# Output stores of the first four token tiles go into the queue six steps later

## The chip, the cores and the metric

The kernel runs on one core of one Trainium2 chip. The metric is the device time of one execution in microseconds; lower is better. Before the change the median of three runs is 2676.28 us, the runs lying from 2673.13 to 2678.49 us. All arithmetic is in fp32; every large matrix product is split into high and low fp32r parts and issued as three matmuls.

## The reference, cut to what matters

One transformer layer on 1024 latent tokens and 256 context tokens, width 1024: a half-step SwiGLU, two parallel attentions with a gated output projection, and a second half-step SwiGLU. The change touches the very last piece, the down projection of the second SwiGLU and the residual step that writes the output:

```python
def _rmsnorm(x, g):
    x32 = x.astype(jnp.float32)
    y = x32 * lax.rsqrt(jnp.mean(x32 * x32, axis=-1, keepdims=True) + RMS_EPS)
    return y.astype(x.dtype) * g

def _residual(x, y, g_post, gate, weight):
    return x + weight * gate * _rmsnorm(y, g_post)

def _swiglu(h, w1, w3, w2):
    return (jax.nn.silu(h @ w1) * (h @ w3)) @ w2
...
        x = _residual(x, _swiglu(_modnorm(x, g[4], m[6], m[7]), ffn2_w1[l], ffn2_w3[l], ffn2_w2[l]),
                      g[5], m[8], HALF_STEP)
    return x
```

## The kernel before, in words

The program is fully unrolled. It is written as a list of *steps* (class `Plan`): each step has one main piece of work, mostly matmuls, and side pieces that `plan.spread` hangs on chosen steps. All that a step issues is recorded in that order, and since nearly every instruction is pinned, each engine runs its own instructions in exactly the recorded order. An instruction that has to wait holds up whatever stands behind it on the same engine.

All transfers, loads and stores alike, go through one queue, SP's. `ld` puts a load at the end of the queue at once. `store(dst, src, n)` does not: it notes the store and puts it into the queue at the end of the step that comes `n` steps later (`flush` does this after each step).

The last phase is the second SwiGLU's down projection, class `Down7`: 77 products, each a 128-deep slice of one of seven sums (a Strassen-Winograd scheme with seven blocks of 11 products). Products 0 to 71 are steps *o* to *o*+71 here. Each has four groups of three matmuls of 128x512, one group per PSUM bank (the names `bs`, `bm`, `bv`). The last five products, 72 to 76, are done bank by bank in four tail steps. Called "product *i*" below, each needs:

- a load of two tiles of 128x512 (named `t`, from scratch tensors `d`), put into the queue six steps ahead (`load`); for products 72 to 76 this is at steps *o*+59, 61, 63, 65 and 67. The `t` tiles come from a pool of 20 slots.
- a split of both tiles (`split`) three steps ahead: ScalarE (ACT) casts the high part into `xu`, VectorE (DVE) subtracts for the low part. For products 72 to 76 this is at steps *o*+62, 64, 66, 68 and 70.

At the end of a block of 11 products `out` adds the banks into the result tiles `ys` (name `xv`) on DVE. Block 4 ends with step *o*+54, block 5 with *o*+65; blocks 5 and 6 gather in the same four banks.

After step *o*+54 the rows of token tiles 0 to 3 are complete, and `done2(t, 0)` and `done2(t, 1)` finish them at steps *o*+55+2t and *o*+56+2t. The first loads the residual rows of the tile from scratch tensor `x2s` into a 128x1024 tile (`xr` in the code, `xv<-d` in a profile), computes the row's inverse norm (a square with a sum on ACT, two tiny operations on POOL) and multiplies by the gate row on DVE (`z`). The second does one DVE SCALAR_TENSOR_TENSOR, z times the inverse norm plus `xr`, and stores z to `out` (`out_x<-xv`). Token tiles 4 to 7 follow in the same way in the tail steps.

Of the kernel before, what the change touches and what calls it, by code (L numbers as in the profile page):

```python
# [15 lines left out]
P = 128  # L16
# [27 lines left out]
def hybrid_block(ctx: ExitStack, tc: tile.TileContext, a: dict, out: bass.AP):  # L44
# [25 lines left out]
    def V(dt=F32):  # L70
        return U(dt, "v")
# [50 lines left out]
    def ld(dst, src):  # L122
        for x in [x for x in waiting if x[1].tensor.name == src.tensor.name]:
            waiting.remove(x)
            put(*x[1:])
        return put(dst, src)
# [4 lines left out]
    def put(dst, src):  # L131
        return pin(nc.sync.dma_start(dst, src))  # L132

    def store(dst, src, n=2):

        if clock[0] is None:
            return put(dst, src)
        waiting.append((clock[0] + n, dst, src))
# [218 lines left out]
    def rstd(src, n):  # L357
        junk = T2(BF16, 1024)
        ss = ST()
        act.activation(junk[:, :n], src, AF.Square, accum_out=ss)  # L360
        r = ST()
        pool.tensor_scalar(ss, ss, 1.0 / n, EPS, op0=ALU.mult, op1=ALU.add)
        pool.tensor_tensor(r, ss, mhalf[:, 0:1], op=ALU.pow)
        return r
# [703 lines left out]
    o = len(plan.main)  # L1068
# [57 lines left out]
    o = len(plan.main)  # L1126
# [6 lines left out]
    for i, d in enumerate(downs):  # L1133
        last = i == len(downs) - 1
        o = len(plan.main)
# [18 lines left out]
        if i < len(downs) - 2:  # L1154
            n = downs[i + 1]
            plan.spread([lambda n=n: n.loads(n.fs[0])], o, o + 1)
            plan.spread(n.steps(), o + 3, e)
        elif not last:
            n = downs[i + 1]
# [87 lines left out]
    o = len(plan.main)  # L1247
# [144 lines left out]
    o = len(plan.main)  # L1392
# [5 lines left out]
    for x, (c, s, ts) in enumerate(sets):  # L1398
        o = len(plan.main)
# [211 lines left out]
    o = va_at  # L1611
# [10 lines left out]
    o = len(plan.main)  # L1622
# [3 lines left out]
    o = len(plan.main)  # L1626
# [4 lines left out]
    o = len(plan.main)  # L1631
# [3 lines left out]
    o = len(plan.main)  # L1635
# [379 lines left out]
    for d in range(KD):  # L2015
        o = len(plan.main)
# [51 lines left out]
    o = len(plan.main)  # L2068
# [13 lines left out]
    o = len(plan.main)  # L2082
# [14 lines left out]
    o, tail = down2.plan(plan)  # L2097
# [8 lines left out]
    def done2(t, x):  # L2106
        y = ys2[t]
        if x == 0:
            xr, r, z = V(), rstd(y, D), V()
            ld(xr, x2s[t * P:(t + 1) * P, :])  # L2110
            vec.tensor_tensor(z, y, cols["g8"], op=ALU.mult)
            cols[t] = xr, r, z
        else:
            xr, r, z = cols[t]
            n = 512 if t == 7 else D
            for o in range(0, D, n):
                vec.scalar_tensor_tensor(z[:, o:o + n], z[:, o:o + n], r, xr[:, o:o + n], op0=ALU.mult, op1=ALU.add)
                store(out[t * P:(t + 1) * P, o:o + n], z[:, o:o + n], 0)

    plan.spread(ada_steps((8,)), o + 1, o + 2 * NP - 3)  # L2120
    plan.spread([last_col], o + 2 * NP - 3, o + 2 * NP - 2)
# [1 line left out]
    for t in range(4):  # L2123
        plan.spread([lambda t=t, x=x: done2(t, x) for x in range(2)], o + 5 * NP + 2 * t, o + 5 * NP + 2 * t + 2)
        plan.spread([lambda t=t: done2(t + 4, 0)], tail + t, tail + t + 1)
        plan.spread([lambda t=t: done2(t + 4, 1)], min(tail + t + 1, tail + 3), tail + 4)
# [79 lines left out]
```

## Time and profile before

| What | Value |
|---|---|
| Median of three runs | 2676.28 us |
| Profiled execution, its own time | 2674.99 us |
| Span of that execution, first to last instruction | 2672.9 us |
| PE (TensorE matmuls) busy | 2612.1 us, 98% of the span |
| DVE busy | 1847.6 us, 69% |
| ACT busy | 1173.5 us, 44% |
| POOL busy | 229.5 us, 9% |
| Mean granted TensorE clock | 0.992 |

Times are in microseconds from the start of the span. Engine rows give when an instruction, or a run of alike ones, begins and how long it lasts; in square brackets stands the idle time of the engine ahead of it, and the engine and tile whose work ended that idle time. `SPq` rows are the moments at which SP issues a transfer, not the transfer itself. DVE instructions overlap a little in the record, so what one costs in a row of them is the distance between starts.

### The profile page before, as it was taken

What the parts mean: (1) busy time and instruction counts of PE and PEld (TensorE: products, weight loads), DVE (VectorE), ACT (ScalarE), POOL (GpSimd) and SP (SyncE); (2) the same over time, 40 slices, a digit from 0 to 9 for tenths busy, and PEclk for the clock granted to TensorE, in tenths of its full rate; (3) what the DMA queues carried; (4) which work ended last, traced back from release to release, by engine and by line L of the source; (5) the groups of instructions that cost most, each with busy time, mean ns of one, the idle gap of its engine ahead of it and who ended that gap; (6) DMA issues with size and microseconds to landing.
All of it is one profiled execution on the core that took longest, in us unless ns stands there. A gap on an engine that the chain in (4) does not pass through costs nothing. (4 is left out here: it accounts for less than half of the span.)

```text
span 2672.9 us, 38325 instructions
## 1 busy us (share of the span) xinstructions
PE 2612.1 (98%) x13690; PEld 2235.5 (84%) x13690; DVE 1847.6 (69%) x3495; ACT 1173.5 (44%) x2248; POOL 229.5 (9%) x380
## 2 busy tenths in 40 slices
PE   7999999999999999999999999999999999999997
PEld 5888888888888788789888999997788888888885
DVE  4777875586866676665466988886525788777555
ACT  4532223532223663331346988774246322234533
POOL 0000000000000400000102432221011000000001
PEclk9999999999999999999999999999999999999998
DMA  7454433453433564477789942214325566557645
GB/s 288 154 165 144 143 117 114 143 169 107 167 109 107 196 229 155 158 245 237 216 285 275 254 115 74 74 30 172 108 87 186 196 229 224 181 186 268 225 162 200
DMA packets 220430, 460.58 MB, mean 172 GB/s; under 512 B 25488, under 2 KB 64592, under 8 KB 220240
## 3 DMA queue, kind: packets, MB, share of 16 engines
q1 hardware_dynamic: 220240, 458.14, 52.2%
q8 instruction: 108, 1.77, 0.3%
q14 instruction: 82, 0.67, 0.1%
HBM read 338.71 MB, written 119.34 MB: 171 GB/s over the span
## 5 line engine op out<-in xcount | busy, mean ns | idle before, releaser
L153 PE MATMUL bm<-xu,xu 128*128 128x512 f32 (+1 forms) x2271 | 553.9, 388 | 1.4 <-DVE xu L120 1.1
L153 PEld LDWEIGHTS bm<-xu,xu 128*128 128x128 f32 x2271 | 420.2, 189 | 84.2 <-DVE xu L120 1.9
L153 PE MATMUL bs<-xu,xu 128*128 128x512 f32 (+1 forms) x1875 | 462.5, 386 | 10.6 <-DVE xv L120 8.5
L120 ACT CAST xu<-t 128x512 fp32r<-128x512 f32 x402 | 239.5, 618 | 407.4 <-DVE t L120 333.7
L153 PEld LDWEIGHTS bs<-xu,xu 128*128 128x128 f32 x1875 | 348.3, 189 | 79.1 <-issue 8.9
L120 DVE TENSOR_TENSOR xu<-t,xu 128x512 fp32r<-128x512 f32 x402 | 265.8, 686 | 142.8 <-ACT xu L120 142.8
L153 PE MATMUL bs<-xv,xu 128*128 128x512 f32 (+1 forms) x1488 | 356.0, 389 | 5.1 <-DVE t L120 5.0
L153 PEld LDWEIGHTS bs<-xv,xu 128*128 128x128 f32 x1488 | 279.5, 189 | 62.9 <-issue 7.1
L153 PE MATMUL bv<-xv,xu 128*128 128x512 f32 x1276 | 318.5, 389 | 0.0
L153 PEld LDWEIGHTS bv<-xv,xu 128*128 128x128 f32 x1276 | 239.5, 188 | 49.9
L120 POOL TENSOR_SCALAR st<-st 128x1 f32<-128x1 f32 x72 | 39.4, 547 | 2089.1 <-ACT t L120 2029.3
L153 PE MATMUL bs<-w,w 96*128 96x512 f32 (+3 forms) x832 | 206.1, 366 | 7.7 <-DVE st L1725 7.1
L120 DVE TENSOR_TENSOR xu<-xu,xu 128x512 fp32r<-128x512 f32 (+2 forms) x219 | 149.3, 687 | 76.9 <-ACT xu L120 75.2
L153 PE MATMUL bm<-t,xu 128*128 128x256 f32 (+1 forms) x1272 | 167.4, 289 | 0.6 <-ACT t L120 0.4
L153 PEld LDWEIGHTS bm<-t,xu 128*128 128x128 f32 x1272 | 162.3, 193 | 5.7 <-ACT t L120 0.8
L120 DVE TENSOR_TENSOR xu<-xv,xu 128x512 fp32r<-128x512 f32 (+2 forms) x184 | 131.3, 738 | 48.2 <-ACT xu L120 45.0
L120 DVE TENSOR_TENSOR t<-t,t 128x512 f32<-128x512 f32 (+2 forms) x222 | 142.3, 643 | 25.8 <-ACT t L120 23.0
L153 PE MATMUL bv<-t,w 128*128 128x256 f32 x896 | 151.2, 288 | 4.9 <-ACT t L1859 1.7
L153 PEld LDWEIGHTS bv<-t,w 128*128 128x128 f32 x896 | 132.6, 189 | 20.6 <-DVE t L1860 5.0
L153 PE MATMUL bv<-xu,xu 128*128 128x512 f32 x530 | 144.2, 393 | 0.0
L120 ACT CAST xu<-xu 128x512 fp32r<-128x512 f32 (+2 forms) x211 | 127.8, 617 | 28.9 <-DMA xu<-in_wc 22.0
L153 PEld LDWEIGHTS bs<-w,w 96*128 96x128 f32 (+1 forms) x832 | 123.2, 190 | 17.0 <-DVE st L1725 10.1
(192 smaller groups left out, 3585.1 us busy)
## 6 DMA issues: line engine op xcount, KB each, us to landing
d<-t SPq DMA_DIRECT2D x321, 256.0 KB, 2.4
t<-d SPq DMA_DIRECT2D x204, 256.0 KB, 5.0
xu<-in_f1w SPq DMA_DIRECT2D x64, 512.0 KB, 4.0
xv<-in_f1w SPq DMA_DIRECT2D x64, 512.0 KB, 3.7
xu<-in_f2w SPq DMA_DIRECT2D x58, 512.0 KB, 4.6
t<-in_wada SPq DMA_DIRECT2D x112, 256.0 KB, 3.9
w<-d SPq DMA_DIRECT2D x112, 256.0 KB, 6.5
xv<-d SPq DMA_DIRECT2D x42, 512.0 KB, 5.4
```

What stands on the lines that cost most here:

```text
L120: return lambda *x, **y: pin(f(*x, **y))
L153: return pin(nc.tensor.matmul(o, s, m, start=start, stop=stop, skip_group_check=open_group[0]))
```

## The change

The store of token tiles 0 to 3 is handed the number 6 where it was 0. It is thus put into SP's queue at the end of step *o*+62+2t and no longer at the end of *o*+56+2t. Nothing is computed otherwise, and the stores of tiles 4 to 7 keep the number 0.

```diff
             n = 512 if t == 7 else D
             for o in range(0, D, n):
                 vec.scalar_tensor_tensor(z[:, o:o + n], z[:, o:o + n], r, xr[:, o:o + n], op0=ALU.mult, op1=ALU.add)
-                store(out[t * P:(t + 1) * P, o:o + n], z[:, o:o + n], 0)
+                store(out[t * P:(t + 1) * P, o:o + n], z[:, o:o + n], 6 if t < 4 else 0)
```

The two listings below are SP's queue from the place at which the first store stood. In a row stand destination, source and shape, and behind them the semaphores that the transfer waits for: `DMAHW` is an earlier transfer (the eighth before it), `DVE` and `Activation` are an instruction of that engine. Tiles `t_5020` and `t_5021` belong to product 63, `t_5029` and `t_5030` to 64, `t_5033` and `t_5034` to 65, `t_5035` and `t_5036` to 72; `xv_5022` and `xv_5037` are the residual rows of token tiles 1 and 2, and `xv_5013` and `xv_5026` are the z of tiles 0 and 1. Before:

```order
L132 DMA out_x<-xv_5013_25273 128x1024 [waits DMAHW5_49,DVE_49]
L132 DMA t_5020_25318<-d_4027_19719 128x512 [waits DMAHW6_49,Activation_49]
L132 DMA t_5021_25319<-d_4031_19723 128x512 [waits DMAHW7_49,Activation_49]
L132 DMA xv_5022_25322<-d_4021_19713 128x1024 [waits DMAHW0_49]
L132 DMA t_5029_25350<-d_4027_19719 128x512 [waits DMAHW1_49,Activation_49]
L132 DMA t_5030_25351<-d_4031_19723 128x512 [waits DMAHW2_49,Activation_49]
L132 DMA out_x<-xv_5026_25329 128x1024 [waits DMAHW3_49,DVE_49]
L132 DMA t_5033_25374<-d_4027_19719 128x512 [waits DMAHW4_49,Activation_49]
L132 DMA t_5034_25375<-d_4031_19723 128x512 [waits DMAHW5_49,Activation_49]
L132 DMA t_5035_25378<-d_4024_19716 128x512 [waits DMAHW6_49,Activation_49]
L132 DMA t_5036_25379<-d_4032_19724 128x512 [waits DMAHW7_49]
L132 DMA xv_5037_25382<-d_4021_19713 128x1024 [waits DMAHW0_49]
```

And with the change, from the same place:

```order
L132 DMA t_5020_25317<-d_4027_19719 128x512 [waits DMAHW5_49,DVE_49]
L132 DMA t_5021_25318<-d_4031_19723 128x512 [waits DMAHW6_49,DVE_49]
L132 DMA xv_5022_25321<-d_4021_19713 128x1024 [waits DMAHW7_49]
L132 DMA t_5029_25349<-d_4027_19719 128x512 [waits DMAHW0_49,DVE_49]
L132 DMA t_5030_25350<-d_4031_19723 128x512 [waits DMAHW1_49,DVE_49]
L132 DMA t_5033_25372<-d_4027_19719 128x512 [waits DMAHW2_49,DVE_49]
L132 DMA t_5034_25373<-d_4031_19723 128x512 [waits DMAHW3_49,DVE_49]
L132 DMA t_5035_25376<-d_4024_19716 128x512 [waits DMAHW4_49,Activation_49]
L132 DMA t_5036_25377<-d_4032_19724 128x512 [waits DMAHW5_49,DVE_49]
L132 DMA xv_5037_25380<-d_4021_19713 128x1024 [waits DMAHW6_49]
```

The two stores have left this stretch, and the residual rows of tiles 1 and 2 stand behind loads of `t` tiles alone. Those loads now wait for DVE where they waited for ACT: each needs a slot of the `t` pool, and the slot it gets is freed by the DVE half of an earlier split (product 53 for the first, 54 for the second, 57 for `t_5036`). `t_5035` takes the slot that the square of token tile 0 used, so it waits for ACT in both.

The second place is where the stores now stand. Here `xv_5052` is the residual rows of tile 3, `t_5059` to `t_5060` belong to product 68, `t_5065` to `t_5068` to 69 and 74, `t_5071` and `t_5072` to 70. Before:

```order
L132 DMA xv_5052_25442<-d_4021_19713 128x1024 [waits DMAHW0_49]
L132 DMA t_5059_25470<-d_4024_19716 128x512 [waits DMAHW1_49,Activation_49]
L132 DMA t_5060_25471<-d_4032_19724 128x512 [waits DMAHW2_49,Activation_49]
L132 DMA out_x<-xv_5056_25449 128x1024 [waits DMAHW3_49,DVE_49]
L132 DMA t_5065_25500<-d_4024_19716 128x512 [waits DMAHW4_49,Activation_49]
L132 DMA t_5066_25501<-d_4032_19724 128x512 [waits DMAHW5_49,Activation_49]
```

With the change:

```order
L132 DMA xv_5052_25439<-d_4021_19713 128x1024 [waits DMAHW5_49]
L132 DMA t_5059_25467<-d_4024_19716 128x512 [waits DMAHW6_49,DVE_49]
L132 DMA t_5060_25468<-d_4032_19724 128x512 [waits DMAHW7_49,Activation_49]
L132 DMA out_x<-xv_5013_25273 128x1024 [waits DMAHW0_49]
L132 DMA t_5065_25497<-d_4024_19716 128x512 [waits DMAHW1_49,DVE_49]
L132 DMA t_5066_25498<-d_4032_19724 128x512 [waits DMAHW2_49,DVE_49]
L132 DMA t_5067_25501<-d_4024_19716 128x512 [waits DMAHW3_49,DVE_49]
L132 DMA t_5068_25502<-d_4032_19724 128x512 [waits DMAHW4_49,DVE_49]
L132 DMA t_5071_25523<-d_4024_19716 128x512 [waits DMAHW5_49,DVE_49]
L132 DMA t_5072_25524<-d_4032_19724 128x512 [waits DMAHW6_49,Activation_49]
L132 DMA out_x<-xv_5026_25328 128x1024 [waits DMAHW7_49]
```

The store of tile 0 now stands where that of tile 3 stood, and six load transfers lie between it and the store of tile 1. The first store needs no wait for DVE of its own any more, since a load ahead of it waits for a later DVE instruction. On PE, ACT, DVE and POOL the instructions stand in the order they had.

## The prediction

> **What bounds the kernel now.** I read the page's head first, then PE's waits, and from the only long one of them back through DVE to SP's queue.
>
> ```profile
> PE 2612.1 (98%) x13690; PEld 2235.5 (84%) x13690; DVE 1847.6 (69%) x3495; ACT 1173.5 (44%) x2248; POOL 229.5 (9%) x380
> ```
>
> PE is the bound: 98% busy. A change to transfers can gain only where PE stands still. PE's waits in the last 273 us (engine, tile, who ended the wait: us in total, times, longest):
>
> ```profile
> PE bs L153 <- DVE xv L120: 8.5, 1, 8.5
> PE bs L153 <- DVE xu L120: 1.3, 1, 1.3
> ```
>
> There are just two, both behind DVE, and PE's timeline has them inside the stretch in which the four stores go out:
>
> ```profile
> 2592.29 0.84 PE L153 MATMUL bs<-xu,xu 128*128 128x512 f32 x3
> ...
> 2621.07 0.84 PE L153 MATMUL bs<-xu,xu 128*128 128x512 f32 x3
> ...
> 2632.46 1.62 PE L153 MATMUL bs<-xu,xu 128*128 128x512 f32 x3 [8.51 <-DVE xv L120]
> ...
> 2637.24 0.85 PE L153 MATMUL bs<-xu,xu 128*128 128x512 f32 x3
> ...
> 2650.87 3.56 PE L153 MATMUL bs<-xu,xu 128*128 128x512 f32 x15
> ```
>
> These rows are the starts of products 55, 65, 66 and 67 and of the tail, whose first row is 15 matmuls on one bank. From 2637.24 to 2650.87 lie five products without a wait, 2.72 us each. From 2592.29 to 2650.87 lie 17, or 46.24 us of work in 58.58 us: 12.34 us are lost. I place them by the rows: product 65 should end at 2621.07 + 2.72 = 2623.79, and 66 starts 8.67 later; 66 takes 4.78 us instead of 2.72, so 2.06 more (its matmuls run slower after the pause); products 55 to 64 take 28.78 instead of 27.2, so 1.6 for the wait of 1.3.
>
> Why DVE is late is in its timeline and its one wait for a transfer between 2592 and 2632:
>
> ```profile
> 2563.18 13.32 DVE L120 TENSOR_TENSOR xu<-t,xu 128x512 fp32r<-128x512 f32 x22
> ...
> 2593.09 2.49 DVE L120 TENSOR_TENSOR xu<-t,xu 128x512 fp32r<-128x512 f32 x4
> 2595.50 1.22 DVE L120 TENSOR_TENSOR xv<-xv,xv 128x1024 f32<-128x1024 f32 x1
> 2596.64 1.29 DVE L120 TENSOR_TENSOR xu<-t,xu 128x512 fp32r<-128x512 f32 x2
> 2597.85 1.27 DVE L120 SCALAR_TENSOR_TENSOR xv<-xv,st,xv 128x1024 f32<-128x1024 f32 x1
> 2599.04 1.28 DVE L120 TENSOR_TENSOR xu<-t,xu 128x512 fp32r<-128x512 f32 x2
> ...
> 2631.64 0.68 DVE L120 TENSOR_TENSOR xv<-xv,bs 128x512 f32<-128x512 f32 x1
> ```
>
> ```profile
> DVE xv L120 <- DMA xv<-d: 13.3, 3, 4.9
> ```
>
> Subtractions of splits (`xu<-t,xu`) alternate with the gate product (`xv<-xv,xv`) and the residual step (`xv<-xv,st,xv`). The residual steps of three tiles wait for their residual rows, 13.3 us together, and behind them on DVE stand splits and, at 2631.64, the clearing of block 5's first bank, for which product 66 waits. Why the rows are late is in SP's queue:
>
> ```profile
> 2570.88 0.42 SPq L132 DMA_DIRECT2D xv<-d  x1
> 2571.72 0.92 SPq L132 DMA_DIRECT2D t<-d  x2
> 2599.15 0.34 SPq L132 DMA_DIRECT2D out_x<-xv  x1
> 2599.58 1.20 SPq L132 DMA_DIRECT2D t<-d  x2
> 2600.83 0.48 SPq L132 DMA_DIRECT2D xv<-d  x1
> ...
> 2610.41 0.42 SPq L132 DMA_DIRECT2D xv<-d  x1
> ...
> 2619.88 0.42 SPq L132 DMA_DIRECT2D xv<-d  x1
> ```
>
> SP issues nothing from 2572.6 to 2599.15: the first store stands there and waits for DVE's residual step (2597.85, ends 2599.12). The rows of tile 0 went out ahead of it (2570.88), those of tile 1 only behind it (2600.83), those of tile 2 behind the store of tile 1 (2610.41), those of tile 3 behind that of tile 2 (2619.88). It is a ring of store, load, landing and residual step. A turn takes 9.5 us and feeds two products, 5.44 us of PE.
>
> **The change part by part.** Removed and added: nothing. The same four stores, 0.34 us of SP each, and the same computations. Moved: four stores by six steps, past loads in SP's queue and no other queue.
>
> *What the move takes away.* No residual rows stand behind a store any more, except those of tiles 4 and 5 behind the last one. I work out when each set of rows can now go out, and when DVE wants it, by the rows above. DVE prices: a subtraction of a split 13.32 / 22 = 0.605, the gate product 2596.64 - 2595.50 = 1.14, the residual step 2599.04 - 2597.85 = 1.19.
>
> - Tile 1: behind the loads of product 63, whose slots come free with splits 53 and 54. These lie in the run of 22 subtractions that starts at 2563.18 and holds products 46 to 56; the 17th ends near 2563.18 + 17 x 0.605 = 2573.5. So the rows go out near 2574. Wanted, by the rows above: 2599.04 + 4 x 0.605 + 1.14 = 2602.6.
> - Tile 2: behind the loads of product 72. One takes the slot of the square of token tile 0, the other that of split 57:
>
> ```profile
> 2591.23 1.06 ACT L120 ACTIVATE t<-xv 128x1024 bf16<-128x1024 f32 x1 [19.36 <-DVE xv L120]
> ```
>
>   The square ends at 2592.29, split 57's first half at 2593.7, so the rows go out near 2594.3. How long such transfers took here, the stores among them, says the view of the tile:
>
> ```profile
> DMA to landing us min/median/max: 2.9/5.4/6.6
> ```
>
>   With the longest they land by 2600.9. Wanted: from 2593.09, 14 subtractions, 3 gate products and 2 residual steps later, 8.47 + 3.42 + 2.38 = 14.27, at 2607.4. Slack 6.5 us.
> - Tile 3: behind a load that needs the slot of split 60's first half (2593.09 + 7 x 0.605 + 1.14 + 1.19 = 2599.7). Out near 2600.2, landed by 2606.8, wanted at 2593.09 + 20 x 0.605 + 4 x 1.14 + 3 x 1.19 = 2613.3. Slack 6.5 us.
>
> So all three DVE waits go. DVE then has 26 subtractions (products 57 to 67, 72 and 73), four gate products and four residual steps ahead of block 5's first clearing: 15.73 + 4.56 + 4.76 = 25.05, and reaches it at 2618.1. PE wants it done when product 66 is due, at 2592.29 + 11 x 2.72 = 2622.2; with 0.69 us for the clearing and 0.14 to the next start, DVE may be there as late as 2621.4. DVE has 3.3 us in hand. As a proof of the account: before, 2618.1 + 13.3 = 2631.4, read 2631.64; and 13.3 - 3.3 = 10.0 of lateness on PE, read 8.67 + 1.6 = 10.3, with the 2.06 of slow matmuls on top.
>
> *What the move brings: loads that wait for a DVE split.* This is the added wait. The nearest row is SP's own waits in the last 172 us:
>
> ```profile
> SPq L132 <- DVE xu L120: 48.1, 46, 15.7
> ```
>
> SP waited 46 times for such a slot, up to 15.7 us, and until 2616 PE did not stand still for it. From below it costs nothing; it gains nothing either. From above it costs what loads lose of their lead. Load 68 waits for split 61 (2602.1) and its own split comes at about 2622.9, after the four clearings: a lead of 20 us against a landing of 6.6. Loads 70, 71 and 76 wait for splits 63, 64 and 72 in the same way, by about 2607, 2610 and 2613, and PE wants products 70 at 2633.1, 71 at 2635.8 and the tail at 2638.5. I take 0, by this row. The upper end I keep for the range is in the rivals: the spare lead of some 13 us used up.
>
> *Held buffers and behind the stores.* z of tiles 0 to 2 is held 3 to 5 us longer after its residual step, and no listed instruction waits for its slot in these steps. The rows of tiles 4 and 5, which follow the last store, now go out at about 2615 and are wanted when the tail is under way, after 2640: hidden. The stores themselves end far ahead of the span's end: hidden, at nothing.
>
> *Transfers side by side.* From 2592.3 to about 2616 the queue now has to move 22 `t` loads (256 KB), the rows of tiles 2 to 5 and four stores (512 KB each), 9.96 MB or 415 GB/s. The rows of this case:
>
> ```profile
> 2610.00:2620.00 10.00, 8.72 (x39) 6.90 (x38) 5.33 (x8) 3.70 (x6) 0.95 (x2) 1.00 0.77 275
> 2620.00:2632.00 12.00, 3.95 (x18) 2.94 (x16) 7.10 (x12) 3.70 (x7) 0.00 (x0) 0.77 0.72 251
> 2632.00:2638.00 6.00, 5.54 (x16) 4.44 (x17) 6.00 (x11) 4.35 (x8) 0.00 (x0) 0.61 1.01 338
> ```
>
> The last three numbers are granted clock, busy share of the transfer engines and GB/s: 338 GB/s at a share of 1.01 is all they did. At that rate the 9.96 MB take 29.5 us, so the last of them, the rows of tile 5, land near 2622 and not 2616. The rows of tile 3 have 3.1 MB in and ahead of them from 2592.3 on, 9.3 us, that is 2601.6: earlier than the issue times allow anyhow. Cost 0; above, 5.5 us of delay on loads that have 13 in hand. [...]
>
> *Sum.* PE gains 1.6 + 8.67 + 2.06 = 12.3 us, 12.34 by the difference of the two totals. The 2.06 comes with the pause: granted clock is 1.00 in the window up to 2620 and 0.61 from 2632 to 2638. [...] What is late next is nothing on PE: block 5's clearing has 3.3 us in hand. From the tail's start (2650.87) to the end of the span everything is the same chain and stays.
>
> The profiled execution took 2674.99 us, and would take 2674.99 - 12.34 = 2662.65. It lies 1.29 us under the median of the runs, so against the median I say 2676.28 - 12.34 = 2663.94.
>
> **The rivals.**
>
> [...]
> - *The stretch is held by transfers.* Up to and with load 70, 5.77 MB go from 2592.3 on, and PE wants them landed by about 2631.3. It decides below 148 GB/s; at 125 GB/s load 70 is 7 us late and the time is 2671, no change. For it: 415 GB/s are asked. Against: 251 to 338 GB/s in the three rows above.
> - *Slower.* The `t` pool closes into a ring: a load goes only after the split of seven products before, and that split needs its load. A turn is landing plus some 2 us (issue, cast, subtraction) and feeds seven products, 19.0 us of PE. It decides from a landing of 17 us; each us beyond that costs one a turn, and products 63 to 76 are two turns. To be slower than 2681.6, 17.7 us must be lost in them, so landings of 26 us, four times the longest seen. Time then 2682 or more. For it: the 15.7 us that SP once waited for a slot. Against: that wait cost PE nothing.
> - *The change not doing what it says* is out: the queue's listing has the stores where they were sent, and the residual rows ahead of them.
>
> **How the numbers follow.** A measurement tells about 0.2% from no change, 5.35 us, as wide as the three runs lay (2673.13 to 2678.49); so faster means under 2670.9. Forecast (all three DVE waits gone, 2660.8 to 2667): 0.85. New gate, part of the gain: 0.07, still faster. Held by transfers: 0.05. Slower: 0.03. That makes faster 0.92, same 0.05, slower 0.03. The gain can't be above 12.34, so the low end is the forecast less the spread of the runs to the fast side, 3.15, and a little for another chip: 2659.5. The high end takes in the rival of the new gate: 2669.
>
> **What would show it.** After the change, SP's queue has the rows of tile 1 out near 2574 and the first store near 2602 to 2603. DVE's residual steps have no wait for `xv<-d` among tiles 0 to 3, and its clearing of block 5 comes with an idle time ended by PE ahead of it, about 2 us. PE has no wait in products 55 to 71, the tail begins near 2638.5, the granted clock stays at 1.00 from 2600 to 2650. I am wrong if PE still waits for DVE at product 66, if rows land more than 12 us after their issue, or if some other pause opens in products 68 to 76.

## The result and the profile after

The change makes the kernel faster by 0.5%: 2661.94 us median of four runs (2659.93 to 2664.47) against 2675.51 us for four runs of the kernel before (2673.13 to 2678.49). The ratio is 0.9949, 95% interval 0.9932 to 0.9966. The forecast was 2663.9 us. Runs of one kernel lie some 5 us apart, so smaller effects are read from the profiles below and not from medians. The profiled execution took 2662.05 us with a span of 2660.0 us; before it was 2674.99 and 2672.9.

SP's queue in the stretch of the four stores, after the change (start, length of the issue, what is moved, how many in a row):

```profile
2570.28 0.42 SPq L132 DMA_DIRECT2D xv<-d  x1
2571.12 2.29 SPq L132 DMA_DIRECT2D t<-d  x4
2573.70 0.32 SPq L132 DMA_DIRECT2D xv<-d  x1
2574.42 19.11 SPq L132 DMA_DIRECT2D t<-d  x6
2593.58 0.42 SPq L132 DMA_DIRECT2D xv<-d  x1
2594.41 5.06 SPq L132 DMA_DIRECT2D t<-d  x6
2599.53 0.42 SPq L132 DMA_DIRECT2D xv<-d  x1
2601.49 0.80 SPq L132 DMA_DIRECT2D t<-d  x2
2602.34 0.42 SPq L132 DMA_DIRECT2D out_x<-xv  x1
```

The residual rows of tiles 1, 2 and 3 go out at 2573.70, 2593.58 and 2599.53; before it was 2600.83, 2610.41 and 2619.88. All three leave ahead of the first store, which is issued at 2602.34 without a long stand. The stand is still there, but elsewhere: the row of 19.11 us holds the load that needs the slot of token tile 0's square.

DVE from the residual step of tile 1 to the clearing of block 5:

```profile
2601.99 1.28 DVE L120 SCALAR_TENSOR_TENSOR xv<-xv,st,xv 128x1024 f32<-128x1024 f32 x1
...
2606.73 1.28 DVE L120 SCALAR_TENSOR_TENSOR xv<-xv,st,xv 128x1024 f32<-128x1024 f32 x1
...
2612.67 1.28 DVE L120 SCALAR_TENSOR_TENSOR xv<-xv,st,xv 128x1024 f32<-128x1024 f32 x1
2613.87 3.69 DVE L120 TENSOR_TENSOR xu<-t,xu 128x512 fp32r<-128x512 f32 x6
2619.77 0.69 DVE L120 TENSOR_TENSOR xv<-xv,bs 128x512 f32<-128x512 f32 x1 [2.21 <-PE bs L153]
```

No residual step has a wait in brackets. DVE, which came to the clearing as late as 2631.64 before, now stands idle for 2.21 us ahead of it and waits for PE.

PE, products 55 and 66 and the start of the tail:

```profile
2591.69 0.84 PE L153 MATMUL bs<-xu,xu 128*128 128x512 f32 x3
...
2621.61 0.84 PE L153 MATMUL bs<-xu,xu 128*128 128x512 f32 x3
...
2637.93 3.56 PE L153 MATMUL bs<-xu,xu 128*128 128x512 f32 x15
```

From 2591.69 to 2637.93 are 46.24 us, exactly 17 products of 2.72; before it was 58.58. From 2400 us to its end PE has no wait left at all. Of the 12.94 us between the two profiled executions 12.34 lie here, and the other 0.60 were there before product 55 began (2591.69 against 2592.29), where both programs are the same.

### The profile page after: what moved, and what is told of

Same layout as the page of the kernel before. It is cut to its first block, busy times and chain, and to the rows that moved or that the text cites. A ratio compares the mean times of both kernels' runs of the same rounds, so it can differ in the third digit from the quotient of the medians.

```text
span 2660.0 us, 38323 instructions
## 1 busy us (share of the span) xinstructions
PE 2609.1 (98%) x13690; PEld 2234.1 (84%) x13690; DVE 1847.5 (69%) x3495; ACT 1171.9 (44%) x2248; POOL 227.9 (9%) x380
## 4 chain that ended last, share of the span: by engine, by line
PE 53%; issue 33%; DVE 6%; ACT 5%; DMA 2%; POOL 1%; SPq 0%; DVEq 0%; POOLq 0%; ACTq 0%
PE bs L153 24%; PE bm L153 15%; PE bv L153 11%; PE bm L156 2%; ACT xu L1833 1%; DVE t L120 1%; DVE xu L1700 1%; DVE xv L120 1%; ACT t L120 1%; DVE xu L120 1%; POOL st L120 1%; ACT t L1859 1%; ACT xu L120 1%; DVE t L1860 1%; PE bs L156 1%
## 5 line engine op out<-in xcount | busy, mean ns | idle before, releaser
L153 PEld LDWEIGHTS bs<-w,w 96*128 96x128 f32 (+1 forms) x832 | 123.2, 190 | 17.1 <-DVE st L1725 10.1
```

The costliest lines, as they stand in the source:

```text
L153: return pin(nc.tensor.matmul(o, s, m, start=start, stop=stop, skip_group_check=open_group[0]))
```

## The experiments

The theory is the ring: a store that waits for DVE holds up the next tile's residual rows in SP's queue, DVE waits for the rows, and PE waits for what stands behind DVE's wait. Three rivals are tried against it: that the `t` loads behind the store are what comes late; that the stores collide with loads as transfers, so that moving them later helps; and that each of the four stores carries a like share. All were timed in five or more rounds against the kernel before on the same chip. Its medians there were 2674.81 us for the first four and 2676.23 us for the last four.

**One step later is enough.** The stores of the kernel before with the number 1 in place of 6:

```diff
-                store(out[t * P:(t + 1) * P, o:o + n], z[:, o:o + n], 0)
+                store(out[t * P:(t + 1) * P, o:o + n], z[:, o:o + n], 1 if t < 4 else 0)
```

> Stores of token tiles 0 to 3 one step later instead of six. Ring theory (a store that waits for DVE holds up the next tile's residual rows in SP's queue, and DVE, then PE, wait for the rows): one step is enough to put each store behind the next tile's rows, so the rows of tile 1 go out near 2574, those of tile 2 behind the store of tile 0 (near 2602, wanted 2607), those of tile 3 behind the store of tile 1 (near 2607, wanted 2613). DVE waits 0 to 3 us in all against 3.2 us in hand: PE waits at most 1 us, time 2662 to 2663. Rival, the t loads behind the store are what comes late: they are still held until 2599, so the time stays near 2675. Rival, the stores collide with loads in the stretch: they go out when they did before, so again near 2675.

Measured: 2662.32 us, ratio 0.9952 (0.9939 to 0.9964). Its SP queue:

```profile
2575.34 0.32 SPq L132 DMA_DIRECT2D xv<-d  x1
2599.87 0.34 SPq L132 DMA_DIRECT2D out_x<-xv  x1
2600.30 3.15 SPq L132 DMA_DIRECT2D t<-d  x6
2603.51 0.42 SPq L132 DMA_DIRECT2D xv<-d  x1
2604.61 0.34 SPq L132 DMA_DIRECT2D out_x<-xv  x1
2605.00 4.09 SPq L132 DMA_DIRECT2D t<-d  x6
2610.14 0.32 SPq L132 DMA_DIRECT2D xv<-d  x1
```

The first store holds SP as before, from 2575.7 to 2599.87, and the `t` loads behind it go out as late as before. Only the rows of tile 1 have slipped past it (2575.34), and each later set past one store. What DVE and PE still wait, DVE from 2592 to 2632 and PE from 2400 on:

```profile
DVE xv L120 <- DMA xv<-d: 4.4, 2, 2.3
PE bs L153 <- DVE xv L120: 1.1, 1, 1.1
```

DVE's waits of 4.4 us, less the 3.2 in hand (worked out below), are 1.2, and PE waits 1.1. DVE waited longer than the 0 to 3 us expected; the account holds with the size that was measured.

**Residual rows early, stores in their old places.** The rows of tiles 0 to 3 are loaded at step *o*+54, and nothing else is changed in the kernel before:

```diff
-        if x == 0:
-            xr, r, z = V(), rstd(y, D), V()
-            ld(xr, x2s[t * P:(t + 1) * P, :])
+        if x < 0:
+            cols["xr", t] = xr = V()
+            ld(xr, x2s[t * P:(t + 1) * P, :])
+        elif x == 0:
+            xr, r, z = cols["xr", t] if t < 4 else V(), rstd(y, D), V()
+            if t >= 4:
+                ld(xr, x2s[t * P:(t + 1) * P, :])
...
+    plan.spread([lambda t=t: done2(t, -1) for t in range(4)], o + 5 * NP - 1, o + 5 * NP)
```

> The kernel before, stores in their old places, but the residual rows of tiles 0 to 3 are loaded together at step o+54, ahead of all four stores. Ring theory: no residual step waits for its rows, and t loads that are held until each residual step ends (2599, 2604, 2609) still land 4 us or more before their split; PE has no wait of over 1 us, time 2662 to 2663. Rival, the t loads behind the store are what comes late: nothing is changed for them, near 2675. Rival, collision of stores and loads: the stores go out where they did, near 2675.

Measured: 2662.34 us, ratio 0.995 (0.9936 to 0.9964). In the SP queue of this kernel the four rows go out first, then the stores at their old step:

```profile
2569.52 2.58 SPq L132 DMA_DIRECT2D xv<-d  x4
2572.43 2.32 SPq L132 DMA_DIRECT2D t<-d  x4
2598.99 0.34 SPq L132 DMA_DIRECT2D out_x<-xv  x1
```

PE has no wait from 2400 on, and no residual step waits for its rows; DVE waits 0.7 us for one inverse norm. The whole gain is had without moving any store in the queue, and with the first `t` loads behind it out at 2599.42, as late as before (2599.58). That refutes two rivals, the late `t` loads and the collision.

**The stores through another queue.** POOL issues the stores of tiles 0 to 3, at their old steps:

```diff
-                store(out[t * P:(t + 1) * P, o:o + n], z[:, o:o + n], 0)
+                (lambda d, s: pin(nc.gpsimd.dma_start(d, s)) if t < 4 else store(d, s, 0))(out[t * P:(t + 1) * P, o:o + n], z[:, o:o + n])
```

> The kernel before, stores of tiles 0 to 3 at their old steps but issued by POOL on its own queue, which has almost nothing else to do; SP never stands behind a store of these tiles. Ring theory: the same gain as six steps later, 2662 to 2664 (POOL's own cost for issuing is unknown; its inverse norms of tiles 2 and 3 stand behind a store, with some 5 us to spare). Rival, collision: the stores now even start earlier, no gain, near 2675.

Measured: 2662.35 us, ratio 0.9952 (0.994 to 0.9965). The stores go out as soon as DVE is done, and PE has no wait from 2400 on. POOL pays something: the inverse norm behind each store is later, and DVE waits for it a little:

```profile
DVE xv L120 <- POOL st L120: 1.5, 2, 0.7
```

That is within what DVE has in hand, and it shows in the idle time ahead of the clearing, which is 0.6 us here and 2.2 in the changed kernel. The collision of transfers is refuted a second time. The profiled execution was the slowest of five (2667.56 us), but not in this stretch, which takes 46.24 us here too.

**Undoing a part.** In the changed kernel the store of tile 0 goes back to its old place, then those of tiles 0, 1 and 2 (`put` issues at once; `k` is 1 and 3):

```diff
-                store(out[t * P:(t + 1) * P, o:o + n], z[:, o:o + n], 6 if t < 4 else 0)
+                (put if t < k else store)(out[t * P:(t + 1) * P, o:o + n], z[:, o:o + n], *(() if t < k else (6 if t < 4 else 0,)))
```

> The changed kernel with the store of tile 0 alone back at its old place. Ring theory: the rows of tile 1 are late by 3.7 to 4.5 us, those of tiles 2 and 3 no longer; DVE has 3.2 us in hand, so PE loses 0.5 to 1.3 us and no clock: 2662.5 to 2663.5. Rival, each of the four stores carries a like share of the 13 us: 2665.

> The changed kernel with the stores of tiles 0, 1 and 2 back at their old places, so that only the store of tile 3 is moved. Ring theory: no residual rows that count stand behind the store of tile 3, so all three waits return, 13 us on DVE, and PE loses about 12 us: 2674 to 2675, as before the change. Rival, each of the four stores carries a like share: a quarter of the gain stays, 2671.5.

Measured: with tile 0 alone back, 2662.6 us, ratio 0.9959 (0.9947 to 0.9972); with three back, 2673.91 us, ratio 0.9992 (0.9983 to 1.0001), as good as the kernel before. DVE's waits for residual rows, of the first and of the second:

```profile
DVE xv L120 <- DMA xv<-d: 5.6, 2, 4.5
```

```profile
DVE xv L120 <- DMA xv<-d: 12.5, 3, 4.7
```

The first store costs DVE 5.6 us: 4.5 at tile 1, as expected, and 1.0 more at tile 2, where none was expected. PE's stretch (reckoned from its product 55 to its tail) grows by 2.5; 5.6 - 3.2 is 2.4. The profile puts this wait of PE down to ACT:

```profile
PE bs L153 <- ACT xu L120: 2.3, 1, 2.3
```

I read it as the wait for DVE's clearing all the same. The cast that is named ends at 2621.92, within 0.01 us of the clearing, and PE starts at 2622.06, as long behind the clearing (0.15) as in the other kernels (0.14 to 0.15). By the plan's order the cast is product 70's, which product 66 does not need.

With three stores back PE's stretch grows by 11.9. Moving the last store alone brings almost nothing, though it is a quarter of the edit: nothing that counts stands behind it. Like shares of 12.3 would be 3.1 for one store and 9.2 for three; 2.5 is too near to 3.1 to decide, but 11.9 is not 9.2, and that rival falls. It falls by the profile. The median is 2.3 us below that of the kernel before, the interval just reaches 1, and a like share (about 3.1 us) lies inside it.

**DVE made late without any store.** In the changed kernel the gate product of tiles 0 to 3 is computed again into the same tile, once more (`k` = 2) or three times more (`k` = 4):

```diff
-            vec.tensor_tensor(z, y, cols["g8"], op=ALU.mult)
+            for _ in range(k if t < 4 else 1):
+                vec.tensor_tensor(z, y, cols["g8"], op=ALU.mult)
```

> The changed kernel, with the gate product of tiles 0 to 3 computed twice into the same tile (4 x 1.14 = 4.56 us more on DVE ahead of the clearing of block 5, no other difference). By the account that DVE has 3.2 us in hand there: PE loses about 1.4 us and no clock, 2663 to 2664. Rival, PE in this stretch hangs on the transfers and DVE's lateness as such costs nothing until much later: 2662, no wait on PE.

> The changed kernel, with the gate product of tiles 0 to 3 computed four times (12 x 1.14 = 13.7 us more on DVE, nearly the 13.3 us that DVE waited for residual rows before the change). By the account: PE loses 13.7 - 3.2 = 10.5 us, in several pauses of 2 to 4 us, and 0 to 2 us by slow matmuls behind them: 2672.5 to 2674.5, the time before the change without any store in the way. Rival, DVE's lateness costs nothing as such: 2662 to 2665.

Measured: 2664.8 us, ratio 0.9965 (0.9953 to 0.9978), and 2676.78 us, ratio 1.0005 (0.9996 to 1.0014). In the second kernel DVE waits for no load at all between 2592 and 2632, and the time is that of the kernel before. PE's waits in the first kernel and in the second:

```profile
PE bs L153 <- DVE xv L120: 1.6, 1, 1.6
```

```profile
PE bs L153 <- DVE xu L120: 5.2, 3, 2.8
PE bs L153 <- DVE xv L120: 3.9, 1, 3.9
```

Each added product took 1.26 us on DVE in this place (a pair in 2.48 where one took 1.22), so the two kernels add 5.0 and 15.1 us, not 4.56 and 13.7. PE's stretch grew by 1.9 and 13.3 us. The first median lies 0.8 us over the top of what I expected and the second 2.3. The larger price explains 0.4 and 1.4 of that. What else there is in the second median its profile can't show: the execution that was profiled, at 2672.73 us, was the fastest of eleven.

Taken together: what DVE is late by (its waits for rows or for an inverse norm, or the added work), the starts of product 55 and of the tail on PE's timeline of each profile, and what the time between them has beyond 46.24 us:

| Kernel | DVE late by, us | less 3.2 in hand | product 55 | tail | PE loses, us |
|---|---|---|---|---|---|
| Changed | 0 | below 0 | 2591.69 | 2637.93 | 0.0 |
| Stores as late as can be (next experiment) | 0 | below 0 | 2592.70 | 2638.94 | 0.0 |
| Rows early | 0.7 | below 0 | 2592.13 | 2638.37 | 0.0 |
| Stores through POOL | 1.5 | below 0 | 2597.09 | 2643.33 | 0.0 |
| One step later | 4.4 | 1.2 | 2593.02 | 2640.62 | 1.4 |
| Gate product twice | 5.0 | 1.8 | 2592.37 | 2640.47 | 1.9 |
| Tile 0 back | 5.6 | 2.4 | 2589.70 | 2638.48 | 2.5 |
| Tiles 0 to 2 back | 12.5 | 9.3 | 2593.80 | 2651.97 | 11.9 |
| Before | 13.3 | 10.1 | 2592.29 | 2650.87 | 12.3 |
| Gate product four times | 15.1 | 11.9 | 2589.05 | 2648.61 | 13.3 |

Up to 5.6 us PE loses what the account says, within 0.2 us. From 12.5 on it loses 1.4 to 2.6 us more, and there granted clock drops as well: to 0.61 from 2632 to 2638 before, to 0.61 from 2632 to 2640 with three stores back, to 0.84 from 2610 to 2620 with four gate products.

**As late as can be.** With the number 40 for tiles 0 to 3, the stores of all eight tiles go out behind every load of the program. Those of tiles 4 to 7 keep the 0, but `flush` takes the noted stores from the front of their list, so they wait too. (They are nine transfers, as tile 7 goes in two halves.)

```diff
-                store(out[t * P:(t + 1) * P, o:o + n], z[:, o:o + n], 0)
+                store(out[t * P:(t + 1) * P, o:o + n], z[:, o:o + n], 40 if t < 4 else 0)
```

> All eight stores noted so late that they enter the queue only at the end of the program, behind the residual rows of tiles 4 to 7. Ring theory: nothing stands behind a store any more, the stores of tiles 0 to 3 go out near 2617 as soon as the last load is issued, since the queue's order is no clock; no wait on PE, 2661 to 2663. Rival, held buffers: the z of tiles 0 to 3 hold slots that tiles 4 to 7 need, or four more stores pile up at the end (2.1 MB at 387 GB/s, 5.4 us): 2664 to 2668.

Measured: 2663.04 us, ratio 0.9954 (0.9942 to 0.9967). No wait on PE, and nothing gained over six steps:

```profile
2614.16 2.10 SPq L132 DMA_DIRECT2D xv<-d  x4
2616.30 41.95 SPq L132 DMA_DIRECT2D out_x<-xv  x9
```

Being last in the queue, the stores still begin at 2616.30, some 40 us ahead of the end. Nothing piles up there: from the tail's start to the end of the span are 22.06 us, against 22.07 with six steps. All versions that break the ring take the same time within their intervals, so none beats the changed kernel, and with PE free of waits in this stretch none could here.

## Why the prediction was right, point by point

- *The bound and its place.* PE's two waits behind DVE were the place. Both are gone, and the stretch of 17 products takes the 46.24 us that were forecast.
- *The residual rows.* They were put at 2574, 2594.3 and 2600.2 and went out at 2573.70, 2593.58 and 2599.53 in an execution that ran 0.6 us earlier there.
- *What DVE has in hand.* Forecast 3.3 us, with an idle time of about 2 us ahead of the clearing; read 2.21. So DVE was there at 2617.56; PE started product 66 at 2621.61, less the 0.83 us that the clearing and the next start take is 2620.78, and 3.2 us were in hand. The experiments bear it out from both sides: up to 1.5 us of lateness cost PE nothing, and from 4.4 to 5.6 us what goes beyond 3.2 is what it cost, within 0.2 us. From 12.5 us on slow matmuls come on top, at a granted clock of 0.61 to 0.84 in the windows named under the table.
- *The added wait.* SP waited for slots longer than before, and PE for none of it. Rows of the changed kernel, from 2500 on:

```profile
SPq L132 <- DVE xu L120: 56.5, 58, 15.8
...
SPq L132 <- ACT t L120: 14.1, 1, 14.1
```

  The 14.1 us are the new gate, at the slot of token tile 0's square. The high end of the range, 2669, and a chance of 0.07 stood for a loss there that no run shows: in the changed kernel rows and stores landed within 7.7 us, and no residual step waited for its rows.

- *Transfers side by side.* Here a number was off, though not the term. I took 338 GB/s as all that the transfer engines did. That was wrong already for the kernel before: elsewhere in the same trace it moved 412 GB/s from 10 to 20 us, loads alone, and 399 from 1360 to 1370. I had read three windows and taken the highest for a ceiling. The changed kernel also did more (last three numbers: clock, share, GB/s):

```profile
2600.00:2610.00 10.00, 10.00 (x46) 8.29 (x45) 10.00 (x13) 8.22 (x16) 1.14 (x2) 1.00 0.97 335
2610.00:2620.00 10.00, 10.00 (x45) 8.28 (x45) 7.79 (x13) 6.32 (x11) 0.00 (x0) 1.00 1.01 387
```

  Landings of rows and stores grew from 5.4 us at the median and 6.6 at most to these, and were hidden, as the term said; the cost of 0 came true:

```profile
DMA to landing us min/median/max: 3.6/6.5/7.7
```

- *Clock.* 1.00 in both of these windows: the 2.06 us of slow matmuls went with the pause. The sum with 2.06 fits the stretch (12.34).
- *The sum.* 12.34 us forecast, 12.34 in the stretch. That the hundredths agree is no skill: the forecast was the stretch before less 17 whole products, so it had to come out once every wait was gone. What was at risk was that no new wait opens. By the medians the gain is 13.57 us, with 9 to 18 us inside the interval; the excess over 12.34 is not located by any run. The measured median is 2.0 us below the forecast: 1.2 is this excess, and 0.8 came from a fourth run that moved the median before from 2676.28 to 2675.51. Both are inside the spread of the runs.

## What to carry to other kernels

A store at the head of a queue waits for the engine that makes its data, and every load behind it waits as well (before the change SP issued nothing from 2572.6 to 2599.15 us); look for a ring in which such a load feeds the next thing that the same engine has to do. To break the ring it is enough that the one load that matters stands ahead of the store, by moving either of them or by another queue: one step brought here all but 1.4 us of what six brought. Before pricing such an edit, work out how late the engine in between may be before the bound engine feels it: here the margin was 3.2 us, lateness of up to 1.5 was free, lateness of 4.4 to 5.6 cost what lay beyond the margin within 0.2, and lateness of 12.5 to 15.1 cost 1.4 to 2.6 us more, with the granted clock down to between 0.61 and 0.84.

## What the runs showed of the hardware that I had not expected

In these traces the length of a pause of PE does not by itself say whether slow matmuls follow it. In the kernel with four gate products PE paused for 1.28 and later for 2.79 us:

```profile
2607.04 0.73 PE L153 MATMUL bs<-xu,xu 128*128 128x512 f32 x2 [1.28 <-DVE xu L120]
...
2608.31 1.52 PE L153 MATMUL bv<-xu,xu 128*128 128x512 f32 x6
...
2615.56 0.73 PE L153 MATMUL bs<-xu,xu 128*128 128x512 f32 x2 [2.79 <-DVE xu L120]
...
2616.91 2.76 PE L153 MATMUL bv<-xu,xu 128*128 128x512 f32 x6
```

After the pause of 1.28 us six matmuls take 1.52 us as ever; after the one of 2.79 us the first two take 0.73 us, as after the shorter one, and then six take 2.76, at a granted clock of 0.74 and 0.65 in the two windows from 2615.5 to 2621. After a shorter pause, 1.99 us, six matmuls were slow as well, in the kernel with three stores back (first two rows); after a longer one than that, 2.27 us, they were not, in the kernel with tile 0 alone back (last two):

```profile
2620.66 0.84 PE L153 MATMUL bs<-xu,xu 128*128 128x512 f32 x2 [1.99 <-DVE xu L120]
...
2622.58 2.47 PE L153 MATMUL bv<-xu,xu 128*128 128x512 f32 x6
```

```profile
2622.06 0.93 PE L153 MATMUL bs<-xu,xu 128*128 128x512 f32 x3 [2.27 <-ACT xu L120]
...
2623.52 1.52 PE L153 MATMUL bv<-xu,xu 128*128 128x512 f32 x6
```

The six take 2.47 us in the first, where the granted clock was 0.83 from 2620 to 2632, and 1.52 in the second. Pauses of 1.1 us (one step later) and 1.6 us (gate product twice) were followed by six matmuls in 1.52 and 1.54. What decides between 1.99 and 2.27 us no run here isolates.

The rate of transfers in one window is no ceiling, even at a full busy share: at shares from 1.01 to 1.03 the traces have 338 GB/s (before, 2632 to 2638), 387 (changed, 2610 to 2620) and 412 (before, 10 to 20).
